# Attention half of an encoder layer: key products moved to VectorE, transposed outputs staged in a buffer of their own, and copies out of PSUM raised in priority

## The chip, the cores and the metric

The kernel runs on one core of a Trainium2 chip. The metric is the device time of one execution in microseconds (us). Where several executions are given, the number is their median. The engines are called as the profile calls them: PE is TensorE (matmuls), PEld its weight loads, DVE is VectorE, ACT is ScalarE, POOL is GpSimd, and SP is SyncE, whose queue issues nearly all transfers.

## The reference, cut to what matters

One layer with two branches. Branch A is a gated linear attention in chunks of 64 frames, branch B a pooling mixer. The change touches branch A alone.

```python
h = x @ w_in
q, k, v, gate_a, alpha_low, pool_in, gate_b, merge_logits = split(h)
G = cumsum(log_alpha, over the 64 frames of a chunk)
decay = exp(-abs(G_t - G_s))
scores = einsum('bhtd,bhsd,bhtsd->bhts', q, k, decay)       # inside a chunk
o = scores @ v + (q * exp(G)) @ state                       # state over chunks
state = exp(G_last) * state + (k * exp(G_last - G)).T @ v
o = o * rsqrt(mean(o * o) + eps) * g_norm                   # 4 heads, 1024 frames
...                                                         # gates, pooling, projections, layer norm
```

Sizes: 1024 frames, width 1024, 4 heads with 128 key and 256 value channels, all in float32.

## The kernel before

The first part, up to about 370 us, makes the attention output; the second part is a chain of large matrix products and is not touched.

In the first part a loop runs over the four heads `h`. The sum with `decay` is split into six levels: for each of the levels 32, 16, 8, 4, 2 the function `level` builds a factor `e` (two subtractions on DVE, an exponential on ACT), then the decayed queries `qs` = q * e on DVE and the decayed keys `ks` = k * e on POOL (L392). `scores` multiplies them on PE into a bank `ps_s`, and a masked copy (L407; L405 on ACT for level 32) takes them into the tile `Pc`. `single_frames` adds the last level. `place` (L410, L411) copies `Pc` into the tile `P`. `ends` makes, for the next head, the factors to the ends of the chunk, `ke` = k * e1 among them (L321, on POOL). `states` makes the running states `st` (L424 on PE, L429 and L432 on DVE), and `outputs` makes `ps_o` (L441, L443) and copies it back over v (L446). `norm` (L469) scales it, and `out_t` transposes it on DVE in 32x32 blocks into a staging tile `oTs` (L476), which four transfers for each half write to DRAM (L478). The first half of head `h` is staged during the loop step of head `h + 1`.

The staging tile is taken from the tag `E`, which has two buffers and also holds all factors `e`, `e0` and `e1`: a factor that comes after it waits until the transfers of the staging tile are done.

The attention matmuls don't fill PE. Between them the loop places filler: the projections q, k of the next head, the rest of v (`v1_gen`, matmuls of 264 columns, evicted by `keep_v`, L149 and L151), and the eight blocks `la`, which go through the single buffer of the pool `sg` to DRAM (L295, L296). Each projection's weights are split into a high and a low part (`whi` on ACT, `wlo` on DVE, L53) through a ring of four buffers.

The order of each engine's instructions is made when the kernel is built, by a list scheduler that goes by priorities and by its own estimates of times. `tc.high_priority(offset=...)` lets the instructions inside it go ahead of others that are ready. At run time each engine works through its list in order and waits on semaphores.

Of the kernel before, what the change touches and what calls it, by code (L numbers as in the profile page):

```python
# [7 lines left out]
F32 = mybir.dt.float32  # L8
# [4 lines left out]
ALU = mybir.AluOpType  # L13
# [3 lines left out]
P = 128  # L17
# [4 lines left out]
H = 4  # L22
DV = 256
CH = 64
NPR = S // P
# [11 lines left out]
def encoder_layer(ctx: ExitStack, tc: tile.TileContext, xT, x, w_av, w_v, w_blk, w_up, b_al, g_norm,  # L37
                  w_pool, p_scale, b_mrg, w_pa, w_pb, w_o, ln_g, ln_b, ident_c, rcnt_c, masks_c, out):
    nc = tc.nc
    act, dve, pool_e, pe, sp = nc.scalar, nc.vector, nc.gpsimd, nc.tensor, nc.sync  # L40
# [40 lines left out]
    masks = const.tile([P, 5, CH], U8, name="masks")  # L81
# [9 lines left out]
    gla = tc.alloc_tile_pool(name="gla", bufs=1)  # L91
# [36 lines left out]
    v = [c_v.tile([P, D], F32, tag="C", name=f"v_{t}") for t in range(NT)]  # L128
# [14 lines left out]
                        yield n * 0.416 + 3  # L143

    def keep_v(tbs, outs, c0):
        for n, (tb, o) in enumerate(zip(tbs, outs)):
            dst = v[tb][:, c0:c0 + o.shape[1]]
            if n % 2:
                dve.tensor_copy(dst, o)  # L149
            else:  # L150
                act.copy(dst, o)  # L151

    accs = [ps_acc.tile([P, S], F32, tag="acc", name=f"ps_v0_{i}") for i in range(2)]
    scs = [ps_sc.tile([P, 512], F32, tag="sc", name=f"ps_v0_{i}") for i in (5, 6)]
# [84 lines left out]
    for i in (0, 64):  # L239
        dve.tensor_copy(a_nat[:, :, i:i + 16], a_hi.bitcast(F32))  # L240
    keep_v(range(8), [o[:, 16:] for o in a_outs], 0)
    for half in range(2):
        ps = ps_m.tile([P, 512], F32, tag="m", name=f"ps_at{half}")
# [6 lines left out]
    qt, kt_, gt = {}, {}, {}  # L250
# [3 lines left out]
    pt = gla.tile([P, NPR, P], F32, name="P")  # L254
    pc = gla.tile([P, NPR, CH], F32, name="Pc")
    pool_e.memset(pt[CH:, :, :CH], 0.0)

    def pairs(t):
        return t.rearrange("p (b t) -> p b t", t=P)
# [39 lines left out]
    def ends(h):  # L299

        q, k, g = qt[h], kt_[h], gt[h]
        gc = g.rearrange("p (c t) -> p c t", t=CH)
        e0 = gla.tile([P, S], F32, tag="E", name=f"e0_{h}", bufs=2)
        act.activation(e0, g, AF.Exp, scale=1.0 / TAU)
        lastv = e0.rearrange("p (b c t) -> p b c t", c=2, t=CH)[:, :, :, CH - 1:CH]
        egl = gla.tile([P, NPR, 2, 1], F32, tag="egl", name=f"egl_{h}", bufs=2)
        dve.tensor_copy(egl, lastv)
        dec = gla.tile([P, NPR], F32, tag="dec", name=f"dec_{h}", bufs=2)
        dve.tensor_tensor(out=dec, in0=egl[:, :, 0, 0], in1=egl[:, :, 1, 0], op=ALU.mult)
        e1 = gla.tile([P, S], F32, tag="E", name=f"e1_{h}", bufs=2)  # L310
        dve.tensor_tensor(out=e1.rearrange("p (c t) -> p c t", t=CH),
                          in0=gc[:, :, CH - 1:CH].to_broadcast([P, 16, CH]), in1=gc, op=ALU.subtract)
        act.activation(e1, e1, AF.Exp, scale=1.0 / TAU)
        cq = gla.tile([P, 1072], F32, tag="qs", name=f"cq_{h}", bufs=2)
        qc = cq[:, :512].rearrange("p (b t) -> p b t", t=CH)
        pr = cq[:, 512:].rearrange("p (c b n) -> p c b n", c=2, b=NPR)
        ke = gla.tile([P, S], F32, tag="ks", name=f"ke_{h}", bufs=2)
        qp, e0p = pairs(q), pairs(e0)
        by_chunk = lambda t: t.rearrange("p (b c t) -> p c b t", c=2, t=CH)
        qx, kx, ex, kex = by_chunk(q), by_chunk(k), by_chunk(e1), by_chunk(ke)  # L320
        pool_e.tensor_tensor(out=ke, in0=k, in1=e1, op=ALU.mult)  # L321
        dve.tensor_tensor(out=qc, in0=qp[:, :, CH:], in1=e0p[:, :, CH:], op=ALU.mult)
        for c in range(2):
            ev = lambda t: t[:, c].rearrange("p b (t u) -> p b t u", u=2)[:, :, :, 0]
            dve.tensor_tensor(out=pr[:, c, :, :32], in0=ev(qx), in1=ev(kx), op=ALU.mult)
        f62, f63 = slice(CH - 2, CH - 1), slice(CH - 1, CH)
        dve.tensor_tensor(out=pr[:, :, :, 32:33], in0=qx[:, :, :, f62], in1=ex[:, :, :, f62], op=ALU.mult)
        dve.tensor_tensor(out=pr[:, :, :, 32:33], in0=pr[:, :, :, 32:33], in1=kx[:, :, :, f63], op=ALU.mult)
        dve.tensor_tensor(out=pr[:, :, :, 33:34], in0=qx[:, :, :, f63], in1=kx[:, :, :, f63], op=ALU.mult)
        dve.tensor_tensor(out=pr[:, :, :, 34:35], in0=qx[:, :, :, f63], in1=kex[:, :, :, f62], op=ALU.mult)  # L330
        gs[h] = dict(qc=qc, pr=pr, ke=ke, dec=dec, e0=e0, egl=egl)
# [46 lines left out]
    def level(h, hl):  # L378

        g = gt[h]  # L380
        gv = g.rearrange("p (b c t) -> p b c t", c=2, t=hl)
        e = gla.tile([P, S], F32, tag="E", name=f"e_{h}_{hl}", bufs=2)
        ev = e.rearrange("p (b c t) -> p b c t", c=2, t=hl)
        nb = S // (2 * hl)
        ref = gv[:, :, 0, hl - 1:hl].to_broadcast([P, nb, hl])
        dve.tensor_tensor(out=ev[:, :, 0, :], in0=ref, in1=gv[:, :, 0, :], op=ALU.subtract)
        dve.tensor_tensor(out=ev[:, :, 1, :], in0=gv[:, :, 1, :], in1=ref, op=ALU.subtract)  # L387
        act.activation(e, e, AF.Exp, scale=1.0 / TAU)  # L388
        qs = gla.tile([P, S], F32, tag="qs", name=f"qs_{h}_{hl}", bufs=2)
        ks = gla.tile([P, S], F32, tag="ks", name=f"ks_{h}_{hl}", bufs=2)  # L390
        dve.tensor_tensor(out=qs, in0=qt[h], in1=e, op=ALU.mult)  # L391
        pool_e.tensor_tensor(out=ks, in0=kt_[h], in1=e, op=ALU.mult)  # L392
        gs[h][hl] = qs, ks

    def scores(h, hl, li):

        qs, ks = gs[h][hl]
        ps = ps_sc.tile([P, 512], F32, tag="sc", name=f"ps_s{h}_{hl}")
        psv = ps.rearrange("p (b t) -> p b t", t=CH)
        for b in range(NPR):  # L400
            for c in range(2):
                cs = slice(b * P + c * CH, b * P + c * CH + CH)
                pe.matmul(psv[c * CH:c * CH + CH, b, :], lhsT=ks[:, cs], rhs=qs[:, cs], start=True, stop=True)  # L403
        if hl == 32:
            act.copy(pc, psv)  # L405
        else:
            dve.copy_predicated(out=pc, mask=masks[:, li - 1:li, :].to_broadcast([P, NPR, CH]), data=psv)  # L407

    def place(h):
        act.copy(pt[:CH, :, :CH], pc[:CH])  # L410
        dve.tensor_copy(pt[CH:, :, CH:], pc[CH:])  # L411

    def states(h):

# [56 lines left out]
    def out_t(h, half):  # L471

        hs = slice(h * DV, h * DV + DV)
        stage = gla.tile([P, 8, 4, 32], F32, tag="E", name=f"oTs_{h}_{half}", bufs=2)
        for b in range(4):
            dve.transpose(stage[:, :, b, :], v[half * 4 + b][:, hs].rearrange("p (j t) -> p j t", t=32))  # L476
        for i in range(4):
            sp.dma_start(oT_d[h, :, :, i, half * 4:half * 4 + 4, :].rearrange("j d b t -> d j (b t)"),  # L478
                         stage[32 * i:32 * i + 32].rearrange("d j b t -> d j (b t)"))


    def v1_gen(grp, tb0):
        acc = [ps_acc.tile([P, S], F32, tag="acc", name=f"ps_v1_{grp}_{tb0 + i}") for i in (0, 2)]
        tbs = range(tb0, tb0 + 4)
        outs = [acc[i // 2][:, i % 2 * 512:i % 2 * 512 + 264] for i in range(4)]
        yield from v_gen(w_v[grp], 264, f"v{grp}_{tb0}", tbs, outs)
        keep_v(tbs, outs, 496 + grp * 264)
# [15 lines left out]
    sg = tc.alloc_tile_pool(name="sg", bufs=1, side="right")  # L503
    for g in (q_gen(0), z_gen(0), k_gen(0)):
        for _ in g:
            pass
    filler = chain([q_gen(1), z_gen(1), k_gen(1), v1_gen(0, 0), v1_gen(0, 4),
                    z_gen(2), q_gen(2), k_gen(2), v1_gen(1, 0), v1_gen(1, 4),
                    z_gen(3), q_gen(3), k_gen(3)] + [la_gen(j, sg) for j in range(8)])
    ends(0)  # L510
    starts(0)
    for h in range(H):
# [3 lines left out]
        def f():  # L516
            fill(todo / steps)

        level(h, 32)
        if h == 0:  # L520
            fill(5000)
            todo -= 5000
        f()
        scores(h, 32, 0)
        cross_chunk(h)
        level(h, 16)
        f()
        k_transposed(h)
        single_frames(h)
        level(h, 8)  # L530
        f()
        scores(h, 16, 1)
        level(h, 4)
        f()
        scores(h, 8, 2)
        states(h)
        level(h, 2)
        if h:
            out_t(h - 1, 0)
        f()  # L540
        scores(h, 4, 3)
        if h:
            out_t(h - 1, 1)
        f()
        scores(h, 2, 4)
        place(h)
        f()
        if h + 1 < H:
            ends(h + 1)
# [7 lines left out]
    for g in range(2):  # L557
        WO.ahead(g, lambda n, nm: gla.tile([P, 2, 512], F32, tag={"22": "KET", "12": "q", "11": "k", "21": "G"}[n], name=nm,
                                           bufs=1 if n == "22" else 2), dve)
    fill(10400)  # L560
    out_t(H - 1, 0)
    out_t(H - 1, 1)
    fill(1e9)
# [416 lines left out]
    outs = [out_pair(tb) for tb in range(4)]  # L980
    n = len(items) - 10
# [73 lines left out]
```

## Time and profile before

| | |
|---|---|
| median of 3 runs | 973.58 us (972.33 to 977.69) |
| the profiled execution's own time | 975.38 us |
| its span, first to last instruction | 973.6 us |
| mean granted clock of TensorE | 0.986 of full speed |
| PE busy over the span | 932.1 us (96%) |
| DVE busy | 750.7 us (77%) |
| ACT busy | 399.8 us (41%) |
| POOL busy | 111.4 us (11%) |

Busy times are sums of the durations of an engine's instructions. PE's busy time contains stretches at half clock, which count as busy though they do half the work. An engine's idle time costs something only if the engine that sets the end waits for it.

### The profile page before, as it was taken

The numbers are of one execution on the slowest core, as the hardware profiler recorded it, in microseconds if no ns is written. First come the engines' busy times: TensorE is split into PE (matmuls) and PEld (weight loads), VectorE is DVE, ScalarE is ACT, GpSimd is POOL, SyncE is SP. The second block draws the span as 40 slices with busy tenths as digits, with TensorE's granted clock in tenths as the row PEclk, the third lists the DMA queues.
The fourth block names the chain that finished last, engine by engine and source line by source line (L and its number), as shares of the span: only waits on it lengthen the run. The fifth ranks groups of instructions, "written<-read, shape, count | busy, mean of one in ns | idle before, by whom it ended". The sixth has DMA issues, their size and how long they took to land. (4 is left out here: it accounts for less than half of the span.)

```text
span 973.6 us, 13056 instructions
## 1 busy us (share of the span) xinstructions
PE 932.1 (96%) x4744; PEld 755.8 (78%) x4744; DVE 750.7 (77%) x1144; ACT 399.8 (41%) x676; POOL 111.4 (11%) x59
## 2 busy tenths in 40 slices
PE   9999889899899999999999999999999999997995
PEld 6887887787677787788878788888888888775874
DVE  5459969859859655878696878788788887799787
ACT  5155335235142124433333333345562543544571
POOL 1523313313324000000000000000000000000022
PEclk9999999999999999999999999999999999997998
DMA  9931110330513738243212179799596787679254
GB/s 288 331 109 35 51 53 26 77 103 24 151 49 121 261 127 309 103 154 138 98 54 87 53 258 342 284 343 336 177 344 215 256 307 215 209 233 335 76 109 107
DMA packets 84144, 169.14 MB, mean 174 GB/s; under 512 B 11456, under 2 KB 28096, under 8 KB 84080
## 3 DMA queue, kind: packets, MB, share of 16 engines
q1 hardware_dynamic: 83216, 165.16, 49.7%
q0 software_dynamic: 864, 3.15, 1.9%
q8 instruction: 37, 0.61, 0.3%
q14 instruction: 27, 0.22, 0.1%
HBM read 114.80 MB, written 53.48 MB: 173 GB/s over the span
## 5 line engine op out<-in xcount | busy, mean ns | idle before, releaser
L455 POOL TENSOR_TENSOR rsr_ln<-rsa_ln,mhalf 128x2 f32<-128x2 f32 (+1 forms) x5 | 5.1, 1014 | 583.0 <-PE psc_o L634 571.0
L392 POOL TENSOR_TENSOR ks<-k,e 128x1024 f32<-128x1024 f32 x20 | 57.8, 2900 | 77.3 <-ACT e L388 63.1
L123 PE MATMUL ps_la<-xh,whi_la 128*128 128x512 f32 x128 | 51.3, 401 | 0.0
L123 PE MATMUL ps_la<-xh,wlo_la 128*128 128x512 f32 x128 | 51.1, 399 | 0.0
L123 PE MATMUL ps_la<-xl,whi_la 128*128 128x512 f32 x128 | 51.0, 398 | 0.0
L141 PE MATMUL ps_v<-whi_v,xh 128*128 128x264 f32 x128 | 38.4, 300 | 3.6 <-DVE v L149 3.1
L388 ACT ACTIVATE e<-e 128x1024 f32<-128x1024 f32 x20 | 21.1, 1059 | 42.8 <-DVE e L387 39.6
L141 PE MATMUL ps_v<-whi_v,xl 128*128 128x264 f32 x128 | 38.6, 302 | 0.0
L141 PE MATMUL ps_v<-wlo_v,xh 128*128 128x264 f32 x128 | 38.0, 301 | 0.0
L52 ACT CAST whi_gb<-raw_gb 128x512 fp32r<-128x512 f32 x28 | 17.3, 621 | 49.0 <-PE psd_pi L634 14.8
L391 DVE TENSOR_TENSOR qs<-q,e 128x1024 f32<-128x1024 f32 x20 | 33.5, 1674 | 2.1 <-ACT e L388 2.0
L52 ACT CAST whi_lb<-raw_lb 128x512 fp32r<-128x512 f32 x28 | 17.4, 621 | 37.1 <-PE psd_lb L634 9.3
L52 ACT CAST whi_gta<-raw_gta 128x512 fp32r<-128x512 f32 x28 | 17.3, 618 | 33.9 <-PE psd_gta L634 10.1
L52 ACT CAST whi_pi<-raw_pi 128x512 fp32r<-128x512 f32 x28 | 17.4, 620 | 32.6 <-PE psd_gb L634 7.0
L52 ACT CAST whi_pb<-raw_pb 128x512 fp32r<-128x512 f32 x28 | 17.1, 619 | 32.8 <-PE psd_pb L634 11.2
L446 DVE COPY v<-ps_o 128x256 f32<-128x256 f32 x32 | 13.3, 421 | 21.8 <-PE ps_o L443 15.8
L141 PEld LDWEIGHTS ps_v<-whi_v,xh 128*128 128x128 f32 x128 | 25.3, 198 | 4.5 <-DVE v L149 3.4
L123 PEld LDWEIGHTS ps_la<-xh,whi_la 128*128 128x128 f32 x128 | 24.1, 188 | 5.7 <-issue 0.4
L123 PEld LDWEIGHTS ps_la<-xh,wlo_la 128*128 128x128 f32 x128 | 24.1, 188 | 5.4
L403 PEld LDWEIGHTS ps_s<-qs,ks 128*64 128x64 f32 x640 | 20.8, 138 | 9.5 <-issue 9.3
L123 PEld LDWEIGHTS ps_la<-xl,whi_la 128*128 128x128 f32 x128 | 24.1, 188 | 5.3
L52 ACT CAST whi_o<-raw_o 128x512 fp32r<-128x512 f32 x28 | 16.9, 617 | 25.1 <-DVE raw_o L619 8.8
(586 smaller groups left out, 3066.4 us busy)
## 6 DMA issues: line engine op xcount, KB each, us to landing
raw_v<-in_w_v SPq DMA_DIRECT2D x16, 264.0 KB, 2.6
xp<-in_xT SPq DMA_DIRECT2D x8, 512.0 KB, 6.8
oT<-oTs SPq DMA_DIRECT2D x32, 128.0 KB, 2.6
raw_la<-in_w_blk SPq DMA_DIRECT2D x8, 512.0 KB, 3.5
wop<-in_w_o SPq DMA_DIRECT2D x8, 512.0 KB, 4.3
la<-la SPq DMA_DIRECT2D x8, 512.0 KB, 3.6
raw_pi<-in_w_blk SPq DMA_DIRECT2D x16, 256.0 KB, 3.8
raw_gb<-in_w_blk SPq DMA_DIRECT2D x16, 256.0 KB, 2.6
```

Source lines behind the costliest of these rows:

```text
L52: act.copy(hi, src)
L123: pe.matmul(ps[:, half * 512:half * 512 + 512], lhsT=a, rhs=mov(b, k, half), start=(i == 0), stop=(i == 23))
L141: pe.matmul(o, lhsT=sta(a, k, tb), rhs=w(k - k0)[b], start=(k == 0 and i == 0), stop=(k == KB - 1 and i == 2))
L388: act.activation(e, e, AF.Exp, scale=1.0 / TAU)
L391: dve.tensor_tensor(out=qs, in0=qt[h], in1=e, op=ALU.mult)
L392: pool_e.tensor_tensor(out=ks, in0=kt_[h], in1=e, op=ALU.mult)
L403: pe.matmul(psv[c * CH:c * CH + CH, b, :], lhsT=ks[:, cs], rhs=qs[:, cs], start=True, stop=True)
L446: dve.tensor_copy(v[b][:, hs], po)
L455: pool_e.tensor_tensor(out=r, in0=a, in1=mhalf[:, :w], op=ALU.pow)
```

## The change

Three things change in the code. The decayed keys `ks` (20 instructions, one for each of 5 levels and 4 heads) and `ke` (4 instructions) are computed by DVE in place of POOL. The copies out of PSUM in `keep_v`, the copies of scores into `Pc`, and the two copies in `place` are put at a higher priority. The staging tile of `out_t` comes, for heads 0 to 2, from the pool `sg` (one buffer, shared with the `la` blocks) in place of the tag `E`; for head 3 nothing changes there.

```diff
@@ keep_v
-        for n, (tb, o) in enumerate(zip(tbs, outs)):
-            dst = v[tb][:, c0:c0 + o.shape[1]]
-            if n % 2:
-                dve.tensor_copy(dst, o)
-            else:
-                act.copy(dst, o)
+        with tc.high_priority(offset=100):
+            for n, (tb, o) in enumerate(zip(tbs, outs)):
+                dst = v[tb][:, c0:c0 + o.shape[1]]
+                if n % 2:
+                    dve.tensor_copy(dst, o)
+                else:
+                    act.copy(dst, o)
@@ ends
-        pool_e.tensor_tensor(out=ke, in0=k, in1=e1, op=ALU.mult)
+        dve.tensor_tensor(out=ke, in0=k, in1=e1, op=ALU.mult)
@@ level
-        pool_e.tensor_tensor(out=ks, in0=kt_[h], in1=e, op=ALU.mult)
+        dve.tensor_tensor(out=ks, in0=kt_[h], in1=e, op=ALU.mult)
@@ scores
-        if hl == 32:
-            act.copy(pc, psv)
-        else:
-            dve.copy_predicated(out=pc, mask=..., data=psv)
+        with tc.high_priority(offset=100):
+            if hl == 32:
+                act.copy(pc, psv)
+            else:
+                dve.copy_predicated(out=pc, mask=..., data=psv)
@@ place
-        act.copy(pt[:CH, :, :CH], pc[:CH])
-        dve.tensor_copy(pt[CH:, :, CH:], pc[CH:])
+        with tc.high_priority(offset=100):
+            act.copy(pt[:CH, :, :CH], pc[:CH])
+            dve.tensor_copy(pt[CH:, :, CH:], pc[CH:])
@@ out_t
-        stage = gla.tile([P, 8, 4, 32], F32, tag="E", name=f"oTs_{h}_{half}", bufs=2)
+        pool, tag = (sg, "sg") if h < H - 1 else (gla, "E")
+        stage = pool.tile([P, 8, 4, 32], F32, tag=tag, name=f"oTs_{h}_{half}", bufs=1 if h < H - 1 else 2)
```

The new priorities and engines also move the scheduler's lists. The line numbers of the changed kernel are 1 to 4 higher than those of the kernel before.

First place: DVE, head 0, from the decayed queries of level 8 (`qs_8`) to the copy of the scores of level 16 (`Pc<-masks,ps_s_16`). Before:

```order
L391 TENSOR_TENSOR qs_8_847<-q_589,e_8_843 128x1024
L363 COPY_PREDICATED Pc<-masks,ps_e_837 128x8x2
L277 SCALAR_TENSOR_TENSOR G_808<-smask,zm_796 128x1024
L386 TENSOR_TENSOR e_4_883<-G_604 128x128x4
L387 TENSOR_TENSOR e_4_883<-G_604 128x128x4
L386 TENSOR_TENSOR e_2_943<-G_604 128x256x2
L387 TENSOR_TENSOR e_2_943<-G_604 128x256x2
L364 COPY_PREDICATED Pc<-masks,ps_e_837 128x8
L53 TENSOR_TENSOR wlo_v_0_4_0_1072<-raw_v_0_4_1069,whi_v_0_4_0_1071 128x528
L289 COPY k_985<-ps_k_820 128x1024
L391 TENSOR_TENSOR qs_4_887<-q_589,e_4_883 128x1024
L407 COPY_PREDICATED Pc<-masks,ps_s_16_865 128x512
```

The same place in the changed kernel:

```order
L392 TENSOR_TENSOR qs_8_847<-q_589,e_8_843 128x1024
L393 TENSOR_TENSOR ks_8_848<-k_665,e_8_843 128x1024
L278 SCALAR_TENSOR_TENSOR G_808<-smask,zm_796 128x1024
L387 TENSOR_TENSOR e_4_883<-G_604 128x128x4
L365 COPY_PREDICATED Pc<-masks,ps_e_837 128x8
L388 TENSOR_TENSOR e_4_883<-G_604 128x128x4
L53 TENSOR_TENSOR wlo_v_0_4_0_1072<-raw_v_0_4_1069,whi_v_0_4_0_1071 128x528
L387 TENSOR_TENSOR e_2_943<-G_604 128x256x2
L388 TENSOR_TENSOR e_2_943<-G_604 128x256x2
L409 COPY_PREDICATED Pc<-masks,ps_s_16_865 128x512
```

The key product `ks_8` has come in, and the copy of the scores now stands ahead of the copy of `k` and of `qs_4`.

Second place: DVE, end of head 0, around the first eviction of the rest of v (`v_101<-ps_v_0_0`, the odd frames' block; the even one is on ACT). `ps_s_4` and `ps_s_2` are the scores of the last two levels. Before:

```order
L407 COPY_PREDICATED Pc<-masks,ps_s_4_965 128x512
L322 TENSOR_TENSOR cq_1087<-q_793,e_1_1078 128x512
L325 TENSOR_TENSOR cq_1087<-q_793,k_985 128x8x32 x2
L327 TENSOR_TENSOR cq_1087<-q_793,e_1_1084 128x16
L329 TENSOR_TENSOR cq_1087<-q_793,k_985 128x16
L407 COPY_PREDICATED Pc<-masks,ps_s_2_1018 128x512
L328 TENSOR_TENSOR cq_1087<-cq_1087,k_985 128x16
L330 TENSOR_TENSOR cq_1087<-q_793,ke_1088 128x16
L386 TENSOR_TENSOR e_32_1330<-G_808 128x16x32
L149 COPY v_101<-ps_v_0_0_987 128x264
```

In the changed kernel:

```order
L53 TENSOR_TENSOR wlo_v_4_4_0_1244<-raw_v_4_4_1241,whi_v_4_4_0_1243 128x528
L432 SCALAR_TENSOR_TENSOR st_924<-st_924,dec_671,ps_st_4_935 128x256
L150 COPY v_101<-ps_v_0_0_987 128x264
L432 SCALAR_TENSOR_TENSOR st_924<-st_924,dec_671,ps_st_4_935 128x256
L53 TENSOR_TENSOR wlo_v_4_6_0_1305<-raw_v_4_6_1302,whi_v_4_6_0_1304 128x528
L432 SCALAR_TENSOR_TENSOR st_924<-st_924,dec_671,ps_st_6_940 128x256
L150 COPY v_103<-ps_v_0_2_988 128x264
L409 COPY_PREDICATED Pc<-masks,ps_s_4_965 128x512
L322 TENSOR_TENSOR ke_1088<-k_985,e_1_1084 128x1024
```

Both evictions of v now come before the scores of level 4, and `ke` of the next head stands behind them.

On PE the same 4 heads' matmuls and the same filler are issued, but the attention's stand later among the filler: the first output matmul `ps_o` of heads 0 to 3 has 59, 99, 54 and 16 more instructions ahead of it than before, all of them filler moved forward. Between the last score matmul of a head and its first `ps_o` there are now 63, 66, 39 and 29 filler matmuls (before 38, 53, 34 and 31).

## Rows read from the trace of the kernel before

**Rows 1.** Windows of 50 us: busy us (instructions) by engine, granted clock, DMA share, GB/s.

```profile
100.00:150.00 50.00, 44.30 (x374) 40.97 (x373) 40.51 (x61) 18.16 (x39) 14.14 (x6) 0.93 0.17 52
150.00:200.00 50.00, 44.69 (x344) 37.01 (x344) 44.45 (x71) 18.51 (x23) 15.41 (x6) 0.97 0.21 55
250.00:300.00 50.00, 45.21 (x288) 36.46 (x286) 33.42 (x63) 15.94 (x32) 11.79 (x5) 1.00 0.35 107
```

**Rows 2.** PE's waits, 50 to 380 us: total us, times, longest.

```profile
PE ps_o L441 <- ACT P L410: 4.0, 1, 4.0
PE ps_o L441 <- DVE P L411: 3.4, 2, 2.7
PE ps_v L141 <- DVE v L149: 3.1, 1, 3.1
PE ps_s L403 <- DVE egl L307: 2.6, 2, 1.3
PE ps_st L424 <- DVE Pc L407: 2.2, 2, 1.6
PE ps_v L141 <- DVE k L289: 0.5, 1, 0.5
PE ps_s L403 <- DVE Pc L364: 0.5, 1, 0.5
```

**Rows 3.** DVE in order of time: start us, duration us, instruction, [idle before].

```profile
98.05 1.23 DVE L391 TENSOR_TENSOR qs<-q,e 128x1024 f32<-128x1024 f32 x1 [0.24 <-ACT e L388]
...
99.27 4.40 DVE L277 TENSOR_TENSOR_SCAN G<-smask,zm 128x1024 f32<-128x1024 bf16 x1
...
106.06 0.70 DVE L53 TENSOR_TENSOR wlo_v<-raw_v,whi_v 128x528 fp32r<-128x528 f32 x1
106.67 1.21 DVE L289 COPY k<-ps_k 128x1024 f32<-128x1024 f32 x1
107.81 2.27 DVE L391 TENSOR_TENSOR qs<-q,e 128x1024 f32<-128x1024 f32 x1
110.00 0.73 DVE L407 COPY_PREDICATED Pc<-masks,ps_s 128x512 f32<-128x512 uint8 x1
...
122.87 2.40 DVE L322 TENSOR_TENSOR cq<-q,e 128x512 f32<-128x512 f32 x1
...
127.48 0.42 DVE L149 COPY v<-ps_v 128x264 f32<-128x264 f32 x1
...
159.40 2.29 DVE L277 TENSOR_TENSOR_SCAN G<-smask,zm 128x1024 f32<-128x1024 bf16 x1
```

**Rows 4.** POOL in order of time.

```profile
98.09 3.43 POOL L392 TENSOR_TENSOR ks<-k,e 128x1024 f32<-128x1024 f32 x1 [7.46 <-ACT e L388]
...
106.09 6.19 POOL L392 TENSOR_TENSOR ks<-k,e 128x1024 f32<-128x1024 f32 x2 [4.57 <-ACT e L388]
```

**Rows 5.** PE in order of time, around two of its waits.

```profile
110.78 2.04 PE L424 MATMUL ps_st<-v,ket 128*128 128x256 f32 x4 [1.60 <-DVE Pc L407]
...
124.40 0.29 PE L141 MATMUL ps_v<-whi_v,xl 128*128 128x264 f32 x1
124.53 0.28 PE L141 MATMUL ps_v<-wlo_v,xh 128*128 128x264 f32 x1
127.95 0.59 PE L141 MATMUL ps_v<-whi_v,xh 128*128 128x264 f32 x1 [3.15 <-DVE v L149]
```

**Rows 6.** DVE's instructions by line and shape, 50 to 380 us: busy us, mean ns, idle before.

```profile
L391 DVE TENSOR_TENSOR qs<-q,e 128x1024 f32<-128x1024 f32 x20 | 33.5, 1674 | 2.1 <-ACT e L388 2.0
L53 DVE TENSOR_TENSOR wlo_v<-raw_v,whi_v 128x528 fp32r<-128x528 f32 x16 | 15.3, 959 | 2.6 <-ACT whi_v L52 2.5
L53 DVE TENSOR_TENSOR wlo_la<-raw_la,whi_la 128x512 fp32r<-128x512 f32 x16 | 14.2, 885 | 7.1 <-ACT whi_la L52 7.1
L387 DVE TENSOR_TENSOR e<-G 128x512 f32<-128x512 f32 x20 | 13.6, 680 | 0.0
L322 DVE TENSOR_TENSOR cq<-q,e 128x512 f32<-128x512 f32 x4 | 6.0, 1507 | 0.0
```

**Rows 7.** DVE's waits for transfers, 50 to 380 us.

```profile
DVE e L311 <- DMA oT<-oTs: 6.2, 2, 3.5
...
DVE oTs L476 <- DMA oT<-oTs: 4.4, 3, 1.8
```

**Rows 8.** Transfers by line: number, KB each, median us from issue to landing.

```profile
oT<-oTs SPq DMA_DIRECT2D x32, 128.0 KB, 2.6
```

More of the change, by code (lines that the diff above doesn't have):

```diff
@@ L403, in scores @@
                 pe.matmul(psv[c * CH:c * CH + CH, b, :], lhsT=ks[:, cs], rhs=qs[:, cs], start=True, stop=True)
-        if hl == 32:
-            act.copy(pc, psv)
-        else:
-            dve.copy_predicated(out=pc, mask=masks[:, li - 1:li, :].to_broadcast([P, NPR, CH]), data=psv)
+        with tc.high_priority(offset=100):
+            if hl == 32:
+                act.copy(pc, psv)
+            else:
+                dve.copy_predicated(out=pc, mask=masks[:, li - 1:li, :].to_broadcast([P, NPR, CH]), data=psv)
     def place(h):
-        act.copy(pt[:CH, :, :CH], pc[:CH])
-        dve.tensor_copy(pt[CH:, :, CH:], pc[CH:])
+        with tc.high_priority(offset=100):
+            act.copy(pt[:CH, :, :CH], pc[:CH])
+            dve.tensor_copy(pt[CH:, :, CH:], pc[CH:])
     def states(h):
```

## The prediction, on record before the changed kernel was run

> **What bounds the kernel now.** PE does the same matmuls before and after, and it is busy nearly always. So the first thing to read is where PE is not busy in the part that the change touches, the first 370 us. The windows of 50 us show it [rows 1]: of 150 us in the three worst windows PE is idle for 5.7, 5.3 and 4.8 us, 15.8 in all; in the second half of the first part and in the long second part hardly anything is lost that this change could reach. The list of PE's waits names who is late [rows 2]: seven kinds of wait, 16.3 us in total. Every releaser is a copy or a small product on DVE, or the copy of P on ACT, which itself waits for DVE's scores. So PE sets the time, and DVE's lateness is what holds it up.
>
> The second loss is the clock. The granted clock of the windows at 100 and 150 us is 0.93 and 0.97 [rows 1], which is 0.07 x 50 + 0.03 x 50 = 5.0 us of work not done. What PE did before it fell can be read at two places [rows 5]: it had waited 1.6 and 3.15 us, and the next 264-column matmul took 0.59 in place of 0.28 us. So these 5.0 us hang on the waits. Together 16.3 + 5.0 = 21.3 us is all that a change of order can win here: 973.6 - 21.3 = 952.3 us of span.
>
> **Why DVE is late.** In order of time [rows 3, 4], POOL's `ks` starts at 98.09 and runs 3.43 us; DVE's scan, which starts at 99.27, takes 4.40 us, while the same scan at 159.40 with no POOL product beside it takes 2.29. POOL's pair from 106.09 to 112.28 covers a `qs` of 2.27 us, against 1.23 at 98.05. The groups by shape say the same of the whole stage [rows 6]. Taking the undisturbed durations as 1.23 for `qs`, 0.70 for the 528-column split [rows 3] and 0.68 for 128x512 (the `e` product, which shows 680 ns): `qs` 20 x (1.674 - 1.23) = 8.9 us too long, the splits for v 16 x (0.959 - 0.70) = 4.1, those for la 16 x (0.885 - 0.68) = 3.3, `cq` 4 x (1.507 - 0.68) = 3.3, and the one scan 2.1: 21.7 us that I can show, and other two-input instructions will add to it.
>
> The Trainium skill gives a rule for this (SBUF — State Buffer, section "Who interferes with whom"): a VectorE instruction with two SBUF inputs and a GpSimd instruction that reads SBUF use one pair of ports, and the one that comes second is blocked until the first ends. The trace agrees as far as the scan's 4.40 against 2.29 us goes.
>
> **The change part by part.**
>
> *Keys on DVE.* 24 products of 128x1024. Their duration on DVE is that of `qs`; an instruction starts a little before the one ahead of it ends (106.67 + 1.21 = 107.88, the next starts at 107.81), and the `k` copy of the same size is followed 1.14 us later [rows 3]. Cost: 24 x 1.14 = 27.4 us of DVE. Refund: the stretching goes with POOL's products, at least 21.7 us, so DVE's load rises by at most 5.7 us over four heads; the bound on the other side is no refund at all, +27.4. I take the refund as full and DVE's load as unchanged or a little less, since the unlisted kinds of instruction are stretched as well.
>
> What counts is not the load but when the copies come. I work the first place out (the order of DVE in the section on the change). `qs` of level 8 waits for ACT's exponential and starts at 98.05 in both. Then, changed: `qs` 1.14, `ks` 1.14, scan 2.21, two halves of `e` and a small copy 1.3, split 0.61, two halves of `e` 1.2; the copy of the scores of level 16 starts at 105.7 and ends at 106.3. Before it started at 110.00 [rows 3]: 4.3 us earlier, with the `ks` product included. PE came to its state matmuls at 110.78 - 1.60 = 109.2 and waited 1.60 [rows 5]; without the two waits of 0.5 ahead of them and with some 1.6 us less filler ahead it comes at about 106.6. The wait is gone, with little room.
>
> *Copies at higher priority.* No instruction is added. The largest effect is at the second place: before, the eviction of v at 127.48 was behind both copies of scores and behind `cq`, stretched to 2.40 us [rows 3], and PE stood for 3.15 us [rows 5]. Now it is ahead of them. Summing DVE's list on from 106.3 (the copy of `k` and `e1` at 1.14, `qs` and `ks` of two levels 4.56, one copy of scores 0.62, five steps of the states 1.95, four splits 2.45, two small ones 0.2, the eviction 0.42; 12.5 in all) puts the end of this eviction at about 118.8; PE comes there at 106.6 plus 84 filler matmuls of 264 columns at 0.12 to 0.13 us, their spacing [rows 5], and three pairs of state matmuls at some 0.3 us: about 118. So about 1 us of the 3.15 stays.
>
> *Staging apart from E.* Removes DVE's waits on its transfers, 6.2 + 4.4 = 10.6 us [rows 7]; the first kind sits ahead of the last copies of scores and of P, behind which PE stands for the 4.0 and part of the 3.4 us [rows 2]. What it adds: one buffer, so the second half of a head must wait for the first half's transfer, 2.6 us [rows 8]. In the new list of DVE nine instructions lie between the halves for head 0, some 6 us; nothing is added to DVE's path there. SP issues these transfers in its list between weight loads; the loads behind them are for filler that starts several us later.
>
> *Order on PE.* The first output matmul of heads 0 to 3 has 59, 99, 54 and 16 more filler instructions ahead of it; at 0.12 us and more each this is 7 to 12 us for the first three. DVE's chain per head gains 6 products (6.8 us) and loses about as much in stretching, and 3 us of transfers. So for the two large waits before `ps_o` at the head of the list [rows 2] there is room on both counts.
>
> **The sum.** Waits: 16.3 - 4.5 left (1 at the eviction of v; 3.5 for places that I have not summed, a few tenths in each head) = 11.8. Clock: 5.0 - 1.0 left = 4.0, since no wait of over about 1 us should be left to bring it down. Span 973.6 - 15.8 = 957.8. The profiled execution took 975.38 for that span, 1.8 us over the median; taken from the median of the runs, 973.58 - 15.8 = **958 us**.
>
> **Rivals.**
>
> *DVE becomes the bound (slower).* DVE is busy for 85.0 of the 100 us from 100 to 200 [rows 1]. If the long durations are not POOL's doing, 6 x 1.14 = 6.8 us a head come on top, in a stage where it has 15 idle us in 100, much of it forced. The filler put ahead of `ps_o` then only moves the wait to the scores inside a head. Price: up to 27.4 us, less the 10.6 us of transfers, so about 974 + 17 = 990 at worst and 980 to 985 in the middle. It decides where DVE's sum for a head passes PE's time for it. Against it stands the scan of 4.40 against 2.29 us. The Trainium skill's page Perfetto Trace Analysis (section "Optimizing Scalar/DVE Operations") speaks for it in half a sentence: with a saturated DVE, moving work to GpSimd may make sense; the same paragraph warns that the two share a read port. By the first half the time would be that of this rival. Chance 0.05.
>
> *Half returns.* DVE keeps up on average but is late at places with little room, as the first two above (0.3 us and -1 us): 8 to 9 us of waits stay, with half of the clock. 973.6 - 7.8 - 2.5 = 963. Chance 0.22.
>
> *The single staging buffer binds.* The `la` blocks and both halves of three heads go through one buffer. If each half waits a whole transfer, 2.6 us each [rows 8], six times, DVE stands for 15.6 us in place of 10.6, with the scores of the next level behind it. Then the waits before P stay and only the stretching is won: about 5 us for head 0 with 2.5 of clock, 966 to 972. The nine instructions between the halves speak against it. Chance 0.10.
>
> *All of it returns.* 952 to 954, chance 0.13. The forecast (955 to 961) has 0.50.
>
> **How the numbers follow.** The range takes the forecast, full return, and half return, and reaches into the third rival: 952 to 968. What a measurement of this kernel can tell from no change is about 0.5%, 4.9 us: faster means below 968.7. The forecast, full and half return lie there, and a third of the third rival: 0.88. The rest of it, and the mild end of the first, are the same: 0.08. Slower 0.04.
>
> **What would show each step.** In the profile after: `qs` and `ks` at about 1.22 us each with no long ones, the scan at 2.3 four times, and the `wlo` splits at 0.7; DVE's busy time in the first 370 us within 6 us of before. No DVE wait on the staging transfers but for a few tenths. PE's waits from 50 to 380 us at 3 to 6 us, the longest near 1, and the granted clock of the 100 and 150 us windows at 0.99 or 1.00. The prediction is wrong if PE waits again for `Pc` or `P` for several us, or if DVE is busy without a gap through a whole head, or if SP's queue holds weight loads behind a staging transfer so that `whi` comes late.

## The result and the profile after

The changed kernel takes 951.79 us (median of 4 runs, 951.22 to 952.37) against 975.63 us for the kernel before beside it (4 runs, 972.33 to 978.44): a ratio of 0.9753, 95% interval 0.9723 to 0.9783, so 23.8 us less. The forecast was 958 us in 952 to 968: the sign was right, the time came out 6.2 us lower than said, and the measured median lies 0.2 us below the range. The same kernel, run once more beside other runs, took 953.35 (see the experiments).

The profiled execution took 952.35 us, with a span of 950.6 against 973.6. PE does the same matmuls; its busy share rises to 97%. The line of the page with the engines' sums:

```profile
PE 926.2 (97%) x4744; PEld 752.7 (79%) x4744; DVE 738.3 (78%) x1168; ACT 401.5 (42%) x676; POOL 43.0 (5%) x35
```

The windows that answer to [rows 1], with the same columns:

```profile
100.00:150.00 50.00, 49.81 (x423) 44.72 (x422) 41.60 (x75) 22.16 (x43) 2.04 (x1) 1.00 0.19 57
150.00:200.00 50.00, 50.00 (x418) 45.06 (x418) 44.79 (x79) 20.83 (x35) 0.00 (x0) 1.00 0.29 81
250.00:300.00 50.00, 50.00 (x343) 40.83 (x340) 38.79 (x75) 16.64 (x34) 3.21 (x1) 1.00 0.32 100
```

PE loses 0.2 us here where it lost 15.8, and the granted clock is 1.00 in all three. DVE does not do less work in a window; it is busy for more of it, 125 us in these 150 against 118, since the heads' work now goes through in less time. PE's waits from 50 to 380 us, against seven kinds and 16.3 us in [rows 2]:

```profile
PE psc_gb L638 <- DVE wlo_gb L53: 0.6, 1, 0.6
PE ps_v L141 <- DVE v L150: 0.2, 1, 0.2
```

The first of the two already belongs to the part behind the attention. DVE by line and shape, answering to [rows 6]; the last number ahead of the idle time is the mean duration in ns:

```profile
L392 DVE TENSOR_TENSOR qs<-q,e 128x1024 f32<-128x1024 f32 x20 | 24.3, 1214 | 2.3 <-ACT e L389 1.5 <-PE ps_s L404 0.8
...
L387 DVE TENSOR_TENSOR e<-G 128x512 f32<-128x512 f32 x20 | 13.7, 684 | 0.0
L53 DVE TENSOR_TENSOR wlo_v<-raw_v,whi_v 128x528 fp32r<-128x528 f32 x16 | 11.2, 702 | 2.1 <-ACT whi_v L52 2.0
L53 DVE TENSOR_TENSOR wlo_la<-raw_la,whi_la 128x512 fp32r<-128x512 f32 x16 | 11.0, 689 | 6.7 <-ACT whi_la L52 6.7
```

`qs` fell from 1674 to 1214 ns, the splits from 959 and 885 to 702 and 689. And the two places that the prediction worked out, DVE and PE in order of time, answering to [rows 3, 5]. DVE:

```profile
97.89 1.22 DVE L392 TENSOR_TENSOR qs<-q,e 128x1024 f32<-128x1024 f32 x1
99.03 1.22 DVE L393 TENSOR_TENSOR ks<-k,e 128x1024 f32<-128x1024 f32 x1
100.16 2.28 DVE L278 TENSOR_TENSOR_SCAN G<-smask,zm 128x1024 f32<-128x1024 bf16 x1
...
105.44 0.74 DVE L409 COPY_PREDICATED Pc<-masks,ps_s 128x512 f32<-128x512 uint8 x1
...
118.27 0.43 DVE L150 COPY v<-ps_v 128x264 f32<-128x264 f32 x1 [0.15 <-ACT v L152]
```

PE:

```profile
106.75 1.13 PE L427 MATMUL ps_st<-v,ket 128*128 128x256 f32 x4
...
118.75 0.39 PE L141 MATMUL ps_v<-whi_v,xh 128*128 128x264 f32 x1 [0.19 <-DVE v L150]
```

The copy of the scores starts at 105.44 (worked out: 105.7) and PE comes to the states at 106.75 (106.6) without a wait; the eviction of v ends at 118.70 (118.8), and PE, which had come at 118.56, waits 0.19 us.

The clock went with the waits here. Three us behind each of the two old waits, first before, then after:

```profile
112.00:115.00 3.00, 3.00 (x16) 2.82 (x16) 3.00 (x6) 0.63 (x1) 0.28 (x1) 0.62 0.33 90
128.00:131.00 3.00, 3.00 (x14) 3.00 (x15) 2.94 (x5) 1.06 (x1) 1.27 (x1) 0.50 0.10 19
```

```profile
112.00:115.00 3.00, 3.00 (x26) 2.94 (x25) 3.00 (x6) 0.81 (x2) 0.00 (x0) 1.00 0.02 5
128.00:131.00 3.00, 3.00 (x27) 3.00 (x26) 2.93 (x6) 1.69 (x2) 0.00 (x0) 1.00 0.08 11
```

PE is busy for all 3 us in all four rows, but at 0.50, the lower level of 1.2 GHz, it gets 14 matmuls done where it now does 27. The share of busy time alone would have shown nothing.

The first matmul of the part behind (`psa_pi`) starts at 375.79 before and at 353.28 after, with 2,296 matmuls ahead of it in both:

```profile
375.79 0.39 PE L634 MATMUL psa_pi<-xh,whi_pi 128*128 128x512 f32 x1
353.28 0.39 PE L638 MATMUL psa_pi<-xh,whi_pi 128*128 128x512 f32 x1
```

So 22.5 of the 23.0 us of span come from the part that the change touches, and 0.5 from the part behind. 16.3 - 0.2 = 16.1 us of the 22.5 are waits. The clock's share can be added up from narrow windows around the three stretches of the kernel before in which it fell:

```profile
108.00:116.00 8.00, 6.40 (x33) 5.78 (x34) 8.00 (x10) 1.69 (x2) 4.28 (x2) 0.79 0.21 65
124.00:132.00 8.00, 4.85 (x27) 4.64 (x26) 7.94 (x15) 2.96 (x5) 3.00 (x2) 0.79 0.15 50
194.00:200.00 6.00, 3.75 (x13) 3.21 (x14) 5.37 (x12) 2.21 (x3) 1.08 (x2) 0.72 0.20 51
```

That is 8 x 0.21 + 8 x 0.21 + 6 x 0.28 = 5.0 us, and none of it is left after the change. Some 1.4 us of the 22.5 are neither listed waits nor clock; what they are is not shown.

### The profile page after: what moved, and what is told of

It is laid out like the page before. It is cut to its first block, busy times and chain, and to the rows that moved or that the text cites. A ratio compares the mean times of both kernels' runs of the same rounds, so it can differ in the third digit from the quotient of the medians.

```text
span 950.6 us, 13001 instructions
## 1 busy us (share of the span) xinstructions
PE 926.2 (97%) x4744; PEld 752.7 (79%) x4744; DVE 738.3 (78%) x1168; ACT 401.5 (42%) x676; POOL 43.0 (5%) x35
## 5 line engine op out<-in xcount | busy, mean ns | idle before, releaser
L141 PE MATMUL ps_v<-whi_v,xl 128*128 128x264 f32 x128 | 36.5, 286 | 0.0
L53 DVE TENSOR_TENSOR wlo_pi<-raw_pi,whi_pi 128x512 fp32r<-128x512 f32 x28 | 19.2, 686 | 10.3 <-ACT whi_pi L52 10.0
L450 ACT ACTIVATE ps_o<-v 128x256 f32<-128x256 f32 x32 | 12.4, 388 | 32.6 <-DVE v L449 32.6
L392 DVE TENSOR_TENSOR qs<-q,e 128x1024 f32<-128x1024 f32 x20 | 24.3, 1214 | 2.3 <-ACT e L389 1.5
L123 PE MATMUL ps_k<-xh,whi_k 128*128 128x512 f32 x64 | 25.8, 402 | 0.0
```

The costliest lines, as they stand in the source:

```text
L53: (lo_eng or dve).tensor_tensor(out=lo, in0=src, in1=hi.bitcast(F32), op=ALU.subtract)
L123: pe.matmul(ps[:, half * 512:half * 512 + 512], lhsT=a, rhs=mov(b, k, half), start=(i == 0), stop=(i == 23))
L141: pe.matmul(o, lhsT=sta(a, k, tb), rhs=w(k - k0)[b], start=(k == 0 and i == 0), stop=(k == KB - 1 and i == 2))
L450: act.activation(po, v[b][:, hs], AF.Square, accum_out=d["ss"][:, b:b + 1])
```

## The experiments

The theory: POOL's key products stretch the two-input instructions of DVE beside them, DVE's copies come late, and PE waits for them; the clock follows PE's waits. Rival A: what counts is the copies' place in DVE's list. Rival B: the staging transfers hold the scores up. Rival C, against the stretching: a key product takes 2.4 to 3.4 us on POOL and 1.2 on DVE, and it is this delay of `ks` itself that the scores felt.

**One part alone, and two without the keys.** Each undoes the other parts of the diff shown above. The keys alone:

```diff
-        pool_e.tensor_tensor(out=ke, in0=k, in1=e1, op=ALU.mult)
+        dve.tensor_tensor(out=ke, in0=k, in1=e1, op=ALU.mult)
...
-        pool_e.tensor_tensor(out=ks, in0=kt_[h], in1=e, op=ALU.mult)
+        dve.tensor_tensor(out=ks, in0=kt_[h], in1=e, op=ALU.mult)
```

> Only the 24 key products go to VectorE; staging and priorities stay as before. Theory (POOL's products stretch DVE's two-input instructions beside them, so DVE's copies come late and PE waits): qs at 1.22 us in place of 1.67, scan 2.3 four times, DVE's load unchanged; of PE's 16.3 us of waits those behind stretched work go, those behind the 10.6 us of transfers and the late eviction of v stay, about 7 us: 962 to 966. Rival A (the copies' place in DVE's order is what counts): 970 or more, with the waits for Pc and v still there. Rival B (DVE is full and six more products a head cost): 975 to 985.

The priorities alone (the three `with tc.high_priority(offset=100):`):

> Only the copies of scores, P and v are issued earlier; keys stay on POOL, staging in the buffers of E. Theory: POOL's products still stretch DVE's work (qs mean 1.67), so some copies are still late; the wait of 3.15 us for v and perhaps half of the others go: 964 to 969. Rival A (place in the order alone): 953 to 957. Rival B (neither order nor POOL, the staging transfers hold the scores): 970 or more.

The staging alone (the two lines in `out_t`):

> Only the staging of the transposed outputs goes to a buffer apart from E. Theory: DVE's 10.6 us of waits on transfers fall to under 3, PE's waits before the first output matmuls of a head (4.0 and part of 3.4) shrink, the 3.15 for v and the 1.6 for the states of head 0 stay: 967 to 971. Rival B (the staging transfers are the cause of PE's waits): 960 or less. Rival A: no change, 973 to 976.

Priorities and staging, without the keys:

> All but the move of the keys: those stay on POOL. Theory: DVE is still stretched (qs 1.67, one scan 4.4), so 3 to 6 us of PE's waits and part of the clock's 5 us stay: 957 to 963. Rival A (order and staging are enough, POOL's stretching has slack to lie in): 951 to 954, as with all three parts.

Measured beside the same 19 runs of the kernel before (976.64): keys 956.39 (ratio 0.9793, interval 0.9759 to 0.9828), priorities 975.17 (0.9978, 0.9959 to 0.9997), staging 969.94 (0.9941, 0.9917 to 0.9965), priorities with staging 970.03 (0.9933, 0.9903 to 0.9963). So the keys alone bring some 20 us and the staging alone some 6 to 7 (the whole change brings 23.8, so the two overlap); the priorities bring nothing that can be told from no change. Of the theory's ranges the one for the staging held; it gave the priorities too much, alone (964 to 969) and with the staging (957 to 963), and the keys too little (962 to 966).

What the priorities do can be read from the lists alone. With the names' numbers left out, PE, ACT, POOL and SP have the same lists of instructions with and without them, whether the other two parts are there or not. On DVE one early copy of v changes places with the small `a_nat` instruction beside it, ahead of the part that matters. Rival A is therefore not tested by the priorities: they move none of the copies that it speaks of. Moving the keys does lay DVE's list out anew; with the keys alone the eviction of v at place 2 already stands ahead of the scores of level 4. The pair of kernels with POOL's products and fills, below, bears on Rival A. At place 2 PE waits as long as ever with the priorities alone:

```profile
126.64 0.59 PE L141 MATMUL ps_v<-whi_v,xh 128*128 128x264 f32 x1 [3.16 <-DVE v L150]
```

With the keys alone that wait is 0.19 us; the whole first part has one wait of weight left, later, at the eviction of v in the next head (PE's waits from 100 to 200 us, then DVE in order of time):

```profile
PE ps_v L141 <- DVE v L149: 2.8, 2, 2.7
```

```profile
182.72 1.22 DVE L311 TENSOR_TENSOR e<-G 128x1024 f32<-128x1024 f32 x1 [0.79 <-DMA oT<-oTs]
...
187.70 0.43 DVE L149 COPY v<-ps_v 128x264 f32<-128x264 f32 x1
```

A wait of DVE for a staging transfer, 0.79 us, stands 5 us ahead of this eviction; here Rival B can have a part. The staging alone, with the keys on POOL, takes the 4.0 us before P out of PE's waits, but 13.4 us of waits for DVE are left (50 to 380 us; these three are the largest):

```profile
PE ps_st L424 <- DVE Pc L407: 4.3, 4, 1.8
PE ps_v L141 <- DVE v L149: 3.2, 1, 3.2
PE ps_v L141 <- DVE k L289: 2.1, 2, 1.6
```

**The keys with one other part.**

> Keys on VectorE and the copies issued earlier; staging as before. With the keys alone PE still waited 2.7 us for the eviction of v and had 0.97 of the clock in that window, while DVE's 4.9 us of waits on staging transfers cost PE 0.3 us. Theory: the priorities now remove the wait for v and its clock, the staging adds nothing: 951 to 954. Rival (with the keys moved the staging is what still holds): 955 to 957, as with the keys alone.

> Keys on VectorE and staging apart; copies at their old place. Theory: the wait of 2.7 us for the eviction of v and the clock behind it stay, DVE's waits on transfers fall to some 2 us for nothing: 955 to 957. Rival: 951 to 953.

Measured side by side: keys with priorities 955.84 (953.56 to 957.76; ratio 0.98, 0.9764 to 0.9836), keys with staging 953.87 (952.36 to 954.12; 0.9778, 0.9746 to 0.9809). The expectation had it the wrong way round: with the priorities the wait for v stays (2.6 us), with the staging it is gone, and the lists of that kernel are, but for the same pair on DVE, those of the whole change. The step from the keys to keys with staging, 2 us, is at the edge of what this kernel's runs can tell; that the wait of 2.7 us goes is read in the trace. Whether it goes with the transfers or with the new lists that the staging brings along (155 of PE's 4,744 matmuls stand elsewhere) is not separated.

**POOL's products back, with no result that anyone reads.** `ks` stays on DVE; POOL works in the dead buffer of `e` right behind it. One kernel lets POOL repeat the product, the other lets it fill the buffer twice:

```diff
         dve.tensor_tensor(out=ks, in0=kt_[h], in1=e, op=ALU.mult)
+        pool_e.tensor_tensor(out=e, in0=kt_[h], in1=e, op=ALU.mult)
```

> The changed kernel with 20 added products on POOL, k times e into the dead e buffer, right behind the ks product on DVE; nobody needs them but the next user of that buffer, and the result is the same. Theory (POOL's reading stretches DVE): DVE's two-input instructions beside them are long again (two forms of the same shape, mean of qs, splits or e over 1.3 times the undisturbed), DVE's load in 50 to 350 us grows by 15 to 30 us, PE waits 6 to 20 us: 960 to 975. Rival C (what cost was the 3.4 us that ks itself took on POOL, ahead of the scores): durations may stretch but PE does not wait, 951 to 954.

```diff
         dve.tensor_tensor(out=ks, in0=kt_[h], in1=e, op=ALU.mult)
+        for _ in range(2):
+            pool_e.memset(e, 1.0)
```

> The changed kernel with two fills of the dead e buffer by POOL at the same places in place of the products: POOL is busy at the same times but reads nothing. Theory: DVE's durations as in the changed kernel (qs 1.22, split 0.70), 951 to 954. If POOL's mere work or its writes stretch DVE, durations grow as with the products and the time with them, 956 to 975.

With the products 971.03 us (968.85 to 977.04, 10 runs; 0.9957, 0.9934 to 0.998), with the fills 953.84 (952.49 to 954.86, 4 runs; 0.978, 0.9748 to 0.9812): 17.2 us apart, side by side, and both in the range that the theory gave. With the products, DVE by shape:

```profile
L392 DVE TENSOR_TENSOR qs<-q,e 128x1024 f32<-128x1024 f32 x20 | 29.4, 1470 | 1.2 <-ACT e L389 0.8 <-PE ps_s L405 0.4
...
L387 DVE TENSOR_TENSOR e<-G 128x512 f32<-128x512 f32 x20 | 20.0, 1002 | 3.2 <-POOL e L394 3.2
L53 DVE TENSOR_TENSOR wlo_v<-raw_v,whi_v 128x528 fp32r<-128x528 f32 x16 | 17.4, 1096 | 1.1 <-ACT whi_v L52 1.1
L53 DVE TENSOR_TENSOR wlo_la<-raw_la,whi_la 128x512 fp32r<-128x512 f32 x16 | 15.1, 941 | 3.4 <-ACT whi_la L52 3.3
```

Against the changed kernel that is 5.1 + 6.3 + 6.2 + 4.1 = 21.7 us of stretching in four kinds of instruction. In order of time POOL and then DVE:

```profile
100.21 4.22 POOL L394 TENSOR_TENSOR e<-k,e 128x1024 f32<-128x1024 f32 x1 [6.96 <-DVE ks L393]
112.59 2.40 POOL L394 TENSOR_TENSOR e<-k,e 128x1024 f32<-128x1024 f32 x1 [8.15 <-DVE ks L393]
117.35 2.37 POOL L394 TENSOR_TENSOR e<-k,e 128x1024 f32<-128x1024 f32 x1 [2.36 <-DVE ks L393]
```

```profile
102.19 2.80 DVE L387 TENSOR_TENSOR e<-G 128x512 f32<-128x512 f32 x1
...
113.39 2.68 DVE L392 TENSOR_TENSOR qs<-q,e 128x1024 f32<-128x1024 f32 x1
...
117.52 3.38 DVE L53 TENSOR_TENSOR wlo_v<-raw_v,whi_v 128x528 fp32r<-128x528 f32 x2
```

Each long instruction of DVE lies under a product of POOL: 2.80 for 0.68, 2.68 for 1.21, 3.38 for 1.32 (two splits in the changed kernel, 114.18), 5.6 us too much in 19. PE, in order of time, waits about that long a little later:

```profile
124.08 1.97 PE L405 MATMUL ps_s<-qs,ks 128*64 128x64 f32 x32 [5.25 <-DVE st L433]
```

With the fills POOL is at work beside the same instructions and nothing is stretched (POOL, DVE in order of time, DVE by shape):

```profile
110.22 1.97 POOL L395 MEMSET e<- 128x1024 f32 x2 [8.29 <-DVE ks L393]
```

```profile
111.05 1.21 DVE L392 TENSOR_TENSOR qs<-q,e 128x1024 f32<-128x1024 f32 x1
```

```profile
L53 DVE TENSOR_TENSOR wlo_v<-raw_v,whi_v 128x528 fp32r<-128x528 f32 x16 | 11.2, 701 | 1.3 <-ACT whi_v L52 1.3
```

So it is POOL's reading and not its being busy. Nobody reads its result. DVE does wait for the buffer to be free again, but equally in both (3.2 us with the products, 3.1 with the fills), so that is not the difference either. The lists of the two differ a little, since they are laid out anew around POOL's work: 67 of PE's 4,744 matmuls and 34 of DVE's 1,168 instructions stand elsewhere. The difference in time is found in PE's row: the first part ends at 372.29 us with the products and at 355.49 with the fills, 16.8 us apart, and of these 13.6 - 1.9 = 11.7 are PE's waits and 6.5 - 1.5 = 5.0 the clock, by the windows of 50 us. (The profiled execution with the products, 977.04 us, is the slowest of its ten; of the 23.2 us of span between the two profiled executions the other 6.4 lie in the part behind.)

This pair speaks against Rival A as the whole cause: with nearly the same order of the copies, the stretching alone costs 17.2 us. Rival C has little to stand on in the trace of the kernel before: no wait of PE there names POOL, and the one wait of DVE for `ks`, from 50 to 380 us, is

```profile
DVE e L386 <- POOL ks L392: 2.3, 1, 2.3
```

How much the delay of `ks` cost before the change all the same is not measured: the kernel with the products carries both the stretching and the keys on DVE. The Trainium skill says both halves (SBUF — State Buffer, section "Who interferes with whom"): a VectorE instruction with two SBUF inputs contends with a GpSimd instruction that reads SBUF, not with one that only writes it. The traces agree with both: `qs` took 2.68 us beside a product and 1.21 beside a fill.

**Load on DVE without POOL.** The same dead product, but on DVE: at every level (20 of them), or at level 8 alone (4):

```diff
         dve.tensor_tensor(out=ks, in0=kt_[h], in1=e, op=ALU.mult)
+        dve.tensor_tensor(out=e, in0=kt_[h], in1=e, op=ALU.mult)
```

> The changed kernel with one added product per head on VectorE itself (4 of 1.22 us, at level 8, into the dead e buffer): a load on DVE without POOL. If DVE has room for what POOL's stretching cost before, the time stays at 951 to 954; if every us of DVE in a head comes out at the end, 956 to 958.

> The changed kernel with 20 added products on VectorE itself, 20 x 1.14 = 22.8 us more of DVE's time, near the 18 us by which the 20 products on POOL stretched it. Theory (POOL's stretching hurts as lost time of DVE, whatever takes it): PE waits 10 to 20 us, 964 to 975, like the run with POOL's products. Rival C (DVE's load has slack; it is collisions at particular copies that hurt): 953 to 958.

> The changed kernel once more beside these. Its lists of instructions are those of the run with keys and staging (953.87), so the two should agree: 951 to 954. A difference of 2 us is then scatter between runs on the chip.

Side by side: the changed kernel once more 953.35 (952.08 to 956.26; 0.9785, 0.9727 to 0.9843), four products 955.13 (954.04 to 955.48), twenty 963.02 (960.96 to 966.6; 0.9886, 0.9835 to 0.9937). What the four cost can't be told from nothing. The twenty cost 9.7 us for 20 x 1.215 = 24.3 us of DVE, between the two ranges expected. The twenty on POOL cost 17.2; their stretching was 21.7 us in the four kinds, and by the pages DVE is busy for 766.4 us in all with the products and 736.7 with the fills, 29.7 us more. So a us of known work on DVE cost 0.4 us here and a us of stretching some 0.6. That the order of the program is laid out around the first and not around the second would explain it, and is not shown. Nor is DVE's load by itself what made the kernel before slow: with the twenty products its page sum is 761.5 us, more than the 750.7 before the change, and the kernel is still 10 us faster. PE's largest waits with the twenty (50 to 380 us):

```profile
PE ps_la L123 <- ACT la L296: 6.4, 1, 6.4
PE ps_v L141 <- DVE v L150: 2.4, 2, 1.7
```

ACT's copy `la` had stood for 4.9 us for the transfer out of the staging buffer, which it shares. The last run asked whether this buffer is the cost:

```diff
-        pool, tag = (sg, "sg") if h < H - 1 else (gla, "E")
-        stage = pool.tile([P, 8, 4, 32], F32, tag=tag, name=f"oTs_{h}_{half}", bufs=1 if h < H - 1 else 2)
+        stage = gla.tile([P, 8, 4, 32], F32, tag="E", name=f"oTs_{h}_{half}", bufs=2)
```

> The kernel with 20 added products on VectorE (963.02), but with the transposed outputs staged in the buffers of E again, as before the change. In that run PE waited once for 6.4 us, for a copy by ACT that stood 4.9 us for the transfer out of the single staging buffer, which it shares. Theory 1 (the shared buffer costs this, DVE's load does not): no wait for ps_la, 957 to 961, near the run with the keys alone. Theory 2 (DVE's load is what costs, and only shows there): 963 to 970, with other waits in place of this one.

It gave 963.39 (961.18 to 965.52; 0.9883, 0.9821 to 0.9944). The wait for `la` is gone and others have grown (for v 3.0 us in place of 2.4, for two weight splits of ACT that the part behind needs 2.4 and 1.9 in place of 0.7 and 0.8), so the time that theory 1 gave did not come. In the two profiled executions the first part does end earlier without the shared buffer, at 361.51 in place of 365.73 us, and the part behind takes 6.2 us longer, 599.4 in place of 593.2; why is open. The longest wait of a trace was not the price of the thing that it named.

## Why the prediction was right or wrong

*What bounds the kernel.* Right: PE's waits for DVE's late copies, and the clock behind them. The two terms had the right size: of the 16.3 us of waits 16.1 are gone, and the clock's 5.0 us, added up again from narrow windows, are 5.0. The cap was a little low all the same: 952.3 us of span at best, and the span is 950.6. The 1.7 between them are 1.4 us of the first part and 0.5 of the part behind that the prediction had no term for, less the 0.2 of waits that stayed.

*Keys on DVE: cost 27.4, refund taken as full.* Right, and shown from both sides. In the six windows of 50 us from 50 to 350 DVE is busy 229.1 us against 230.2 before; the sums over the six, before and after:

```profile
sum 300.00, PE 283.51 PEld 237.48 DVE 230.21 ACT 116.34 POOL 80.73; mean PE 47.25 PEld 39.58 DVE 38.37 ACT 19.39 POOL 13.45
sum 300.00, PE 299.81 PEld 252.08 DVE 229.07 ACT 122.31 POOL 15.55; mean PE 49.97 PEld 42.01 DVE 38.18 ACT 20.39 POOL 2.59
```

Over the whole execution, which holds the same other work, the refund is more than full: 750.7 + 27.4 - 738.3 gives some 40 us, nearly twice the 21.7 that could be listed. The products that come back on POOL stretch 21.7 us again (the sum of four kinds, not the same four), fills stretch nothing. The durations came out as named: 1.21 to 1.22, 2.28, 0.70.

*Place 1.* Right to 0.3 us.

*Place 2 and "copies at higher priority".* The sum over DVE's list was right to 0.1 us, its reason wrong. The prediction said that the priorities' "largest effect is at the second place" and that the eviction of v "is ahead" of the scores for that. The list had been read with all three parts in it; alone the priorities leave the order as it was and the wait at 3.16 us, and the keys alone put the eviction ahead and bring the wait to 0.19. The rival that ought to have been written down is that one part of the change does nothing. It did not harm the number, since the order was read from the whole change. The 1 us left there was 0.2: PE came at 118.56 instead of 118.

*Staging.* Its 10.6 us of DVE's waits fell to 1.6, as said, and alone it brought some 6 us. The place was only half right: the 4.0 us before P do go, but once the keys are moved, what the staging takes away is a wait of 2.7 us for an eviction of v, and whether it does so by the transfers or by the new lists is open.

*The sum: where it failed.* The step that failed is the remainders, "Waits: 16.3 - 4.5 left" and "Clock: 5.0 - 1.0 left". Measured: 0.2 and, by the three windows, none. Of the 4.5 us, 3.5 were "for places that I have not summed"; no row stood behind them, and the two places that had been summed came out with no wait and one of 0.2. The gain in span was forecast as 15.8 us and is 23.0. Of the 7.2 between them 4.3 are the waits' remainder, 1.0 the clock's, and 1.9 the 1.4 and 0.5 us without a term. With both remainders at nothing the prediction's own working gives 952.3 of span, 1.7 above the 950.6 measured.

*Rivals.* "All of it returns" (952 to 954, chance 0.13) is what happened; the changed kernel gave medians of 951.79 and 953.35, and the kernel without the priorities, whose lists are the same but for one pair on DVE, 953.87. On which side of 952 a median falls is scatter; that hardly any wait is left is not. "Half returns" did not occur. "The single staging buffer binds" did not either: one DVE wait of 1.6 us remains. "DVE becomes the bound" did not occur, and its worst case let every us of added DVE work come out at the end: 27.4 for 27.4, less the transfers. 24.3 us of extra DVE work cost 9.7 us, and the kernel was then still faster than before.

## What to carry to other kernels

When an engine off the bottleneck makes others late, look for the same instruction with and without a neighbour on another engine before counting loads: a product moved from POOL to DVE cost DVE nothing here, since DVE had been paying for it in stretched instructions. Sum every place that waits, or give the remainder the value that the summed places came to; remainders without a row behind them were 4.5 of the 7.2 us of error here. And when several edits change one order, build each alone and compare the lists: an edit that moves no instruction that matters can be struck out before any run.

## What the runs showed of the hardware that was not expected

- The same wait does not always bring the clock down. The kernels with the keys alone and with keys and priorities have the same lists but for one pair of neighbours on DVE; PE waits 2.7 us for v in the one and 2.6 in the other. The 4 us behind it, the keys alone first:

```profile
188.00:192.00 4.00, 3.82 (x22) 3.82 (x23) 3.10 (x9) 1.06 (x1) 0.00 (x0) 0.70 0.39 120
```

```profile
188.00:192.00 4.00, 3.30 (x24) 3.24 (x25) 3.53 (x10) 0.68 (x2) 0.00 (x0) 1.00 0.29 70
```

  The part behind begins 1.9 us later in the first (357.36 against 355.48). What decides it is open.
- The scatter of the kernel before goes with the clock. Of its 46 runs beside the experiments the nine with a mean granted clock of 0.980 to 0.984 have a median of 977.5 us, the eight with 0.990 or 0.991 one of 972.7. Which of the two makes the other is not shown by that.
- With the priorities alone the 95% interval was 0.9959 to 0.9997, with lists that are the same but for two neighbours on DVE. It excludes 1 by 0.0003, which is a reason to keep to the bound of 0.5% that the prediction set itself.
